# Twelve first sums of the down weights under gate and up, read-outs ordered ahead of sums, and plain rows loaded ahead, in a two-layer hybrid encoder

## The chip, the cores and the metric

The kernel runs on one core of one Trainium2 chip. The metric is device time in microseconds (us), the median of the runs; lower is better. In the profile PE is TensorE's matmul and PEld its weight load, DVE is VectorE, ACT is ScalarE, POOL is GpSimd and SP is SyncE, whose queue issues most of the DMAs.

## The reference

The reference is an encoder trunk of two layers on 1024 positions of width 1024, with 16 learned positions put in front (1040 in all). Each layer adds a mixer (a gated delta rule and a short convolution) and then a feed-forward block to the residual. The change lies in the feed-forward block alone:

```python
def swiglu(h, w_gate_up, w_down):
    gate, up = jnp.split(h @ w_gate_up.astype(h.dtype), 2, axis=-1)
    return (jax.nn.silu(gate) * up) @ w_down.astype(h.dtype)
```

Everything is float32. The inner width is 2816, which is 22 rows of 128. The last layer drops the 16 extra positions, so it works on 1024 columns where the first works on 1040.

## The kernel before, in words

**Three matmuls for one.** A float32 matrix is held as two fp32r parts: hi, a rounded copy that ACT makes, and lo, the value minus hi, which POOL makes for weights and DVE for activations. A product is three matmuls, hi by hi, hi by lo and lo by hi (lines 1064 to 1066 for gate and up, 1411 to 1413 for down).

**Seven products for eight.** Both matrix products of the feed-forward block use a Strassen form: the operands are cut into 2 x 2 blocks, and seven products of sums of blocks take the place of eight. For gate and up (the loop over the inner rows `f`, 0 to 21, line 1267) the four weight blocks A11, A12, A21 and A22 of a row are loaded, DVE forms the sums S1 to S4 from them (lines 1277 to 1282), `w_op` (lines 1042 to 1048) makes hi and lo of each, and PE runs p1 to p7. The products leave PSUM on ACT or DVE. Then POOL and DVE scale gate and up, ACT applies SiLU, DVE multiplies (line 1344), and the row goes to DRAM as `ad[f]` (line 1345).

**The down stage.** Down runs over the inner rows. The first four rows (`NF`) are plain: an ordinary product at the very end (`plain_row` prepares their activations, lines 1358 to 1365: load, hi on ACT at 1363, lo on DVE at 1364). The other 18 rows are two halves of nine (`NP`) and go through the seven products. Their work is written as 84 units: product P5, P3, P2, P1, P6, P7, P4 in this order, each with three blocks `b` of three inner rows and four output tiles `m`; a unit is one (product, b, m) with 18 matmuls in the first layer, whose 520 columns are done in two parts, and 9 in the second. A product's weights n = 4b + m are twelve tiles of 128 x 384.

The weights of four products are sums. They are formed in place in twelve half rows `S`:
- the first sum (S1, line 1150) adds two loaded tiles and serves P5;
- the second (S2, line 1152) subtracts a third tile, after P5's weight has been converted, and serves P3 (with one more subtraction, line 1181) and P6;
- the third (S3, line 1154) serves P7.

`s_raw` gives the home of sum n: rows that gate and up no longer need. `s_room` gives the eight half rows into which tiles for first and second sums are loaded: four rows, three that hold `up` and one that holds `gate` of the last products. `w_unit` (lines 1167 to 1186) converts the weight of a unit: hi on ACT (1184), lo on POOL (1185). `t_load` and `t_pair` do the same for the activations of a block (hi on ACT at 1229, lo on DVE at 1230; P7 and P4 need a subtraction first, at 1225 or 1228; at 1232 DVE updates a kept difference). `b_room` hands out seven half rows in turn for loaded activations, two neighbours for a plain row. Tiles with the tag `ck2` come from five buffers, which gate and up use for A21, A22 and two sums of each row and down for raw weights.

**Order.** What is emitted at which unit is written down in the list `under` (lines 1235 to 1247 and 1386 to 1387): weights five units ahead, activations some four, sums at units of their own, plain rows at units 37, 40, 43 and 46. First sums 0 to 7 are emitted by `s_under` behind products 8 to 15 of gate and up, first sums 8 to 11 at units 0 to 3. The emission order is a priority, not the order of execution: the framework simulates the engines' times and puts into each engine's queue, in order, what is ready first. So the first sums that are emitted from product 8 on run from 672.8 us on in the first layer, several products earlier, as soon as their rows are free. On the chip each queue then runs strictly in that order: an instruction that waits holds up all those behind it.

The products take eight PSUM banks in turn. P3 goes on in the banks of P5, P2 takes the next ones in the turn, P1 again the next, and P6, P7 and P4 go on in P1's. In the last block of a product, units 8 to 11 of its twelve, DVE adds the bank to the output rows (the read-out, line 1417), and the next product can write that bank only after it. These are the lines of a unit's end:

```python
                if b == NBK - 1:
                    dh, z, op = TO[p]
                    h = part(hr[4 * dh + m], z, j)
                    tt(out=h, in0=pin(ps), in1=h, op=op)
```

Of the kernel before, what the change touches and what calls it, by code (L numbers as in the profile page):

```python
# [7 lines left out]
F32 = mybir.dt.float32  # L8
# [12 lines left out]
FT = 22  # L21
# [21 lines left out]
def trunk(ctx: ExitStack, tc: tile.TileContext, xT, w_in, w_ba, w_out, w_gu, w_dn,  # L43
# [235 lines left out]
    for l in range(DEPTH):  # L279
# [834 lines left out]
        td = dram.tile([NP, 128, NB], F32, name=nm("td"))  # L1114
        dw = {}
        nr = [0, 0, 0]
        S_UP = 8

# [12 lines left out]
        def s_raw(n):  # L1131
            r = n // 2
            if ("S", r) not in dw:
                dw["S", r] = row(Y[1], F32, 3) if r < 3 else c4k("S") if r < 5 else row(Y[1] + "f")
            return dw["S", r][:, 384 * (n % 2):384 * (n % 2) + 384]

        def s_room():

            nr[2] += 1
            r = nr[2] // 2 % 4  # L1140
            if ("X", r) not in dw:
                dw["X", r] = row(X[1], F32, 3) if r < 3 else row(X[1] + "f")
            return dw["X", r][:, 384 * (nr[2] % 2):384 * (nr[2] % 2) + 384]

        def s_sum(which, n, room=None):

            S = s_raw(n)
            if which == "S1":
                r, o = room or (s_room(), s_room())
                tt(out=S, in0=a_load(r, 1, 0, n), in1=a_load(o, 1, 1, n), op=ALU.add)  # L1150
            elif which == "S2":
                tt(out=S, in0=S, in1=a_load(s_room(), 0, 0, n), op=ALU.subtract)
            else:
                tt(out=S, in0=a_raw(1, 1, n), in1=S, op=ALU.subtract)

        def s_under(f):

            n = f - 8
            if 0 <= n < S_UP:
                s_raw(n)  # L1160
                if n == 0:
                    s_raw(6)
                    s_raw(8)
                dw["S", 4]
                s_sum("S1", n, (dw["S", 4][:, 0:384], dw["S", 4][:, 384:768]))

        def w_unit(u):
# [9 lines left out]
            if p in ("P5", "P6", "P7"):  # L1177
                r = s_raw(n)
            elif p == "P3":
                r = a_raw(0, 1, n)  # L1180
                tt(out=r, in0=r, in1=s_raw(n), op=ALU.subtract)
            else:
                r = a_raw(*{"P2": (0, 1), "P1": (0, 0), "P4": (1, 1)}[p], n)
# [7 lines left out]
        def b_room(n=1):  # L1191

            if n == 2:
                nr[1] += nr[1] % 7 % 2
                if nr[1] % 7 == 6:
                    nr[1] += 1
            c0 = NB * (nr[1] % 7)
            nr[1] += n
            return dw["B"][:, c0:c0 + n * NB]
# [11 lines left out]
        def t_load(t):  # L1211
            p, i = SEVEN[t // NP], t % NP
            if p in BH:
                dw["b", t] = b_load(*BH[p], i)
            elif p == "P5":
                dma(t_raw(i), td[i])

        def t_pair(t):
            p, i = SEVEN[t // NP], t % NP
            hi, lo = t_slot(t)  # L1220
            r = dw.pop(("b", t), None)
            if p in ("P5", "P6"):
                r = t_raw(i)
            elif p == "P7":
                tt(out=r, in0=t_raw(i), in1=r, op=ALU.subtract)
            elif p == "P4":
                b21, r = r, t_raw(i)
                tt(out=r, in0=b21, in1=r, op=ALU.subtract)
            act(out=hi, in_=r, func=AF.Copy)
            tt(out=lo, in0=r, in1=hi.bitcast(F32), op=ALU.subtract)  # L1230
            if p == "P3":
# [5 lines left out]
        for n in range(12):  # L1237
            if n >= S_UP:
                under[n - 8].append(lambda n=n: s_sum("S1", n))
            under[n + 3].append(lambda n=n: s_sum("S2", n))  # L1240
            under[n + 46].append(lambda n=n: s_sum("S3", n))
        for t in range(4, NP * 7):
# [24 lines left out]
        for f in range(FT):  # L1267
# [16 lines left out]
            for n, a in ([("S3", A21), ("A22", A22), ("S4", s2t), ("A12", A12)] if end else  # L1284
                         [("S4", s2t), ("S3", A21), ("A12", A12), ("A22", A22)]):
                if f >= NE or n != "A12":
                    W[n] = w_op(a)
            g, u = early[f] if f < NE else (row((X[1], Y[1])[f % 2] + "f"), row(X[1], F32, 3))
            ps = {}
# [56 lines left out]
            if NF <= f < NF + NP:  # L1346
                tt(out=gv[:, 0:NB].rearrange("p (g e) -> p g e", g=2), in0=half(uv, 1), in1=half(uv, 0), op=ALU.subtract)
                dma(td[f - NF], gv[:, 0:NB])
            s_under(f)

# [5 lines left out]
        rest = []  # L1356

        def plain_row(f):

            u = b_room(2)  # L1360
            dma(u, ad[f][:, o0:L])
            lo = row(X[1], F32R, 3) if f < 3 else row(X[1] + "f", F32R)
            act(out=ax[:, f, o0:L], in_=u, func=AF.Copy)
            tt(out=lo[:, o0:L], in0=u, in1=ax[:, f, o0:L].bitcast(F32), op=ALU.subtract)
            rest.append((ax[:, f, :], lo))
# [20 lines left out]
        for i in range(NF):  # L1386
            under[37 + 3 * i].append(lambda i=i: plain_row(i))
        for u, (p, b, m) in enumerate(UNITS):
            if b == 1 and p in FIRST:
                dh, z = FIRST[p]  # L1390
                q = 4 * dh + m
                dma(half(hr[q][:, o0:L], z), half(hd[q][:, o0:L], z))
            for fn in under[u]:
                fn()
# [9 lines left out]
            for j in range(NJ):  # L1404
# [9 lines left out]
                if b == NBK - 1:  # L1414
                    dh, z, op = TO[p]
                    h = part(hr[4 * dh + m], z, j)
                    tt(out=h, in0=pin(ps), in1=h, op=op)

# [135 lines left out]
```

## Time and profile before

| | |
|---|---|
| runs | 2590.4, 2592.36 and 2598.9 us, median 2592.36 us |
| profiled execution | 2589.49 us, its span 2587.7 us |
| mean granted clock of TensorE | 0.991 |
| DMA | 360.04 MB, mean 139 GB/s |
| gate and up, first layer | from 610.1 us to about 1082 us |
| down, first layer | from 1081.7 us to about 1272 us |
| gate and up, second layer | from 1897.3 us to about 2346 us |
| down, second layer | from 2338.5 us to about 2529 us |

The profile is one execution, recorded by the hardware. The page gives the busy time of each engine over the span. The table by stretches cuts the span and gives for each stretch its length, each engine's busy time with the number of instructions in brackets, the clock that TensorE was granted (1.00 is full), the busy share of the DMA engines and the rate. The list of waits names the waiting instruction, the one that released it, the total, the number of times and the longest. In the timeline by engine a row has start, duration, engine, line, operation and tiles, and in square brackets how long the engine stood idle before it and what ended that. The groups by line give the shortest, the median and the longest duration in ns. Tile names show the buffer's tag: `a` and `b` are the large buffers and the rows `a3` and `b3`, `a3f` and `b3f` the fourth rows, `rw` the ck2 tiles, `S` the row of sums 8 and 9, `P` the buffers of split activations.

### The profile page before, as it was taken

To read this page: it belongs to the slowest core of one execution; us is meant where nothing else is said; L and a number is where in the kernel's file an instruction comes from. 1 tells how busy PE (TensorE), PEld (TensorE's weight loads), DVE (VectorE), ACT (ScalarE), POOL (GpSimd) and SP (SyncE) were. 2 spreads that over 40 slices of the span, in tenths; PEclk is the share of its full clock that TensorE was granted. 3 is DMA by queue.
4 is the path that set the end of the run, shared out by engine and by line. 5 is a ranking of instruction groups with operands and counts; after the bars stand their busy time and mean duration, and the time that the engine had idled before them with its cause. 6 is when DMAs were issued, how large, how long until landed. Compare 5 with 4: busy or idle time off the path is not lost. (4 is left out here: it accounts for less than half of the span.)

```text
span 2587.7 us, 45312 instructions
## 1 busy us (share of the span) xinstructions
PE 2504.7 (97%) x17508; PEld 2289.3 (88%) x17508; DVE 1640.2 (63%) x2461; ACT 1047.0 (40%) x1945; POOL 1134.3 (44%) x869
## 2 busy tenths in 40 slices
PE   8999999999899999999999989999989999999998
PEld 6989999998899999999998978999977778887787
DVE  4588433648766665778455874235587776668754
ACT  5563332435233333444445633324442333333444
POOL 2041212335666666665320302212456776774662
PEclk9999999999999999999999999999999999999999
DMA  3457265524422222674224582556343322228631
GB/s 127 128 184 266 92 206 167 186 78 124 131 98 87 96 83 81 212 221 144 78 92 134 189 269 77 181 159 204 106 133 115 111 88 92 89 82 276 202 109 66
DMA packets 213765, 360.04 MB, mean 139 GB/s; under 512 B 25461, under 2 KB 87869, under 8 KB 213549
## 3 DMA queue, kind: packets, MB, share of 16 engines
q1 hardware_dynamic: 180300, 310.17, 36.8%
q10 hardware_dynamic: 31072, 42.61, 5.4%
q0 software_dynamic: 2176, 4.36, 0.5%
q8 instruction: 137, 2.24, 0.4%
q14 instruction: 80, 0.65, 0.1%
HBM read 266.60 MB, written 90.46 MB: 138 GB/s over the span
## 5 line engine op out<-in xcount | busy, mean ns | idle before, releaser
L130 POOL TENSOR_TENSOR wlo<-raw,whi 128x512 fp32r<-128x512 f32 x132 | 177.5, 1346 | 770.2 <-ACT whi L129 698.4
L156 PE MATMUL pacc<-a,whi 128*128 128x346 f32 (+1 forms) x808 | 264.8, 331 | 9.9 <-ACT whi L129 8.3
L158 PE MATMUL pacc<-a,wlo 128*128 128x346 f32 (+1 forms) x808 | 264.5, 329 | 0.8 <-DVE wlo L130 0.8
L156 PE MATMUL pacc<-b,whi 128*128 128x346 f32 (+2 forms) x672 | 234.8, 350 | 0.0
L158 PE MATMUL pacc<-b,wlo 128*128 128x346 f32 (+2 forms) x672 | 232.5, 348 | 0.0
L157 PE MATMUL pacc<-a,whi 128*128 128x346 f32 (+1 forms) x688 | 227.0, 330 | 0.6 <-DVE a L177 0.3
L129 ACT ACTIVATE whi<-raw 128x512 fp32r<-128x512 f32 x168 | 105.2, 629 | 246.9 <-PE pacc L157 157.1
L157 PE MATMUL pacc<-b,whi 128*128 128x346 f32 (+2 forms) x580 | 200.5, 347 | 0.2 <-DVE b L905 0.2
L1047 POOL TENSOR_TENSOR wlo<-rw,whi 128x512 fp32r<-128x512 f32 x92 | 134.8, 1467 | 72.1 <-ACT whi L1046 66.8
L156 PEld LDWEIGHTS pacc<-a,whi 128*128 128x128 f32 x808 | 154.0, 191 | 13.9 <-ACT whi L129 10.2
L158 PEld LDWEIGHTS pacc<-a,wlo 128*128 128x128 f32 x808 | 154.1, 191 | 2.8 <-DVE wlo L130 1.4
L156 PEld LDWEIGHTS pacc<-b,whi 128*128 128x128 f32 x672 | 127.0, 189 | 11.4 <-issue 3.1
L157 PEld LDWEIGHTS pacc<-a,whi 128*128 128x128 f32 x688 | 131.8, 192 | 5.1 <-issue 2.9
L1047 POOL TENSOR_TENSOR a<-rw,a 128x512 fp32r<-128x512 f32 x64 | 105.6, 1651 | 69.7 <-ACT a L1046 69.0
L158 PEld LDWEIGHTS pacc<-b,wlo 128*128 128x128 f32 x672 | 126.9, 189 | 8.8 <-issue 0.8
L1047 POOL TENSOR_TENSOR b<-rw,b 128x512 fp32r<-128x512 f32 x64 | 92.6, 1449 | 84.2 <-ACT b L1046 50.2
L1046 ACT ACTIVATE whi<-rw 128x512 fp32r<-128x512 f32 x92 | 57.8, 630 | 144.5 <-DVE rw L1281 84.9
L157 PEld LDWEIGHTS pacc<-b,whi 128*128 128x128 f32 x580 | 109.6, 189 | 7.4 <-DVE b L905 0.5
L1282 DVE TENSOR_TENSOR rw<-raw,rw 128x512 f32<-128x512 f32 x44 | 97.2, 2209 | 1.2
L1277 DVE TENSOR_TENSOR rw<-rw,rw 128x512 f32<-128x512 f32 x44 | 67.5, 1533 | 47.3 <-POOL wlo L1047 30.9
L1047 POOL TENSOR_TENSOR wlo<-raw,whi 128x512 fp32r<-128x512 f32 x50 | 79.9, 1600 | 32.0 <-ACT whi L1046 21.3
L1046 ACT ACTIVATE b<-rw 128x512 fp32r<-128x512 f32 x64 | 40.2, 630 | 121.7 <-PE pacc L1065 35.2
(973 smaller groups left out, 8425.1 us busy)
## 6 DMA issues: line engine op xcount, KB each, us to landing
raw<-in_w_in SPq DMA_DIRECT2D x112, 256.0 KB
raw<-in_w_gu SPq DMA_DIRECT2D x104, 256.0 KB
rw<-in_w_gu SPq DMA_DIRECT2D x88, 256.0 KB
rw<-in_w_dn SPq DMA_DIRECT2D x86, 192.0 KB
rec<-aqd SPq DMA_DIRECT2D x62, 256.0 KB
rec<-vkd SPq DMA_DIRECT2D x61, 256.0 KB
raw<-in_w_out SPq DMA_DIRECT2D x48, 256.0 KB
b<-ad SPq DMA_DIRECT2D x45, 260.0 KB
```

Of the source, the lines that this page charges most:

```text
L129: act(out=hi, in_=raw[:, 0:kk, :], func=AF.Copy)
L130: (tt if lov[0] else ptt)(out=lo, in0=raw[:, 0:kk, :], in1=hi.bitcast(F32), op=ALU.subtract)
L156: mm(ps[:, :n], wh, xh[:, n0:n1], start=(k == 0), stop=False)
L157: mm(ps[:, :n], wh, xl[:, n0:n1], start=False, stop=False)
L158: mm(ps[:, :n], wl, xh[:, n0:n1], start=False, stop=(k == K - 1))
L1046: act(out=hi, in_=src, func=AF.Copy)
L1047: ptt(out=lo, in0=src, in1=hi.bitcast(F32), op=ALU.subtract)
L1277: tt(out=s1t, in0=A21, in1=A22, op=ALU.add)
L1282: tt(out=A21, in0=A11, in1=A21, op=ALU.subtract)
```

## The change

It has three parts.

**Twelve first sums under gate and up.** `s_under` is called in each product right after its weights have been prepared, before its matmuls are emitted, where it stood behind the product's end. Sums 8 and 9 are now emitted at products 16 and 17, sums 10 and 11 both at the last product, 21. Sums 8 to 11 load one tile into their own home and the other into a new `ck2` tile, where they took two rooms each. The home of sums 10 and 11 and the fourth row of rooms change places: the home is now the row that holds the gate of product 20 (`X[1] + "f"`), the rooms get the row of product 21's gate.

**Read-outs ahead of sums.** Each unit's read-out is remembered. `behind` adds to an operation of DVE that is emitted at unit u the condition that it runs after the read-out of unit u - 2, if that unit had one: to second and third sums, to the subtractions for P3's weights and for P7's and P4's activations, to the lo parts of activations and of plain rows. Units with a read-out are the last four of each product. Third sums are emitted three units later (n + 49 instead of n + 46).

**Plain rows loaded ahead.** A plain row's load is emitted three units ahead of its conversion, and the conversions stand at units 42, 44, 46 and 70 instead of 37, 40, 43 and 46. `held` keeps, for an assertion, which of the seven half rows are waiting to be read.

The diff, without the assertion's bookkeeping and the blank lines:

```diff
+        at, read_out = [0], {}
+        def behind(ins):
+            return after(ins, read_out.get(at[0] - 2))
-        S_UP = 8
@@ s_raw
-                dw["S", r] = row(Y[1], F32, 3) if r < 3 else c4k("S") if r < 5 else row(Y[1] + "f")
+                dw["S", r] = row(Y[1], F32, 3) if r < 3 else c4k("S") if r < 5 else row(X[1] + "f")
@@ s_room
-                dw["X", r] = row(X[1], F32, 3) if r < 3 else row(X[1] + "f")
+                dw["X", r] = row(X[1], F32, 3) if r < 3 else row(Y[1] + "f")
@@ s_sum
-                tt(out=S, in0=S, in1=a_load(s_room(), 0, 0, n), op=ALU.subtract)
+                behind(tt(out=S, in0=S, in1=a_load(s_room(), 0, 0, n), op=ALU.subtract))
-                tt(out=S, in0=a_raw(1, 1, n), in1=S, op=ALU.subtract)
+                behind(tt(out=S, in0=a_raw(1, 1, n), in1=S, op=ALU.subtract))
@@ s_under
-            n = f - 8
-            if 0 <= n < S_UP:
-                s_raw(n)
+            if f == FT - 1:
+                ns = (10, 11)
+            else:
+                ns = (f - 8,) if 0 <= f - 8 < 10 else ()
+            for n in ns:
+                S = s_raw(n)
                 if n == 0:
                     s_raw(6)
                     s_raw(8)
-                dw["S", 4]
-                s_sum("S1", n, (dw["S", 4][:, 0:384], dw["S", 4][:, 384:768]))
+                if n < 8:
+                    s_sum("S1", n, (dw["S", 4][:, 0:384], dw["S", 4][:, 384:768]))
+                else:
+                    s_sum("S1", n, (S, raw4("ck2").rearrange("p a b -> p (a b)")[:, 0:384]))
@@ w_unit, t_pair
-                tt(out=r, in0=r, in1=s_raw(n), op=ALU.subtract)
+                behind(tt(out=r, in0=r, in1=s_raw(n), op=ALU.subtract))
-                tt(out=r, in0=t_raw(i), in1=r, op=ALU.subtract)
+                behind(tt(out=r, in0=t_raw(i), in1=r, op=ALU.subtract))
-                tt(out=r, in0=b21, in1=r, op=ALU.subtract)
+                behind(tt(out=r, in0=b21, in1=r, op=ALU.subtract))
-            tt(out=lo, in0=r, in1=hi.bitcast(F32), op=ALU.subtract)
+            behind(tt(out=lo, in0=r, in1=hi.bitcast(F32), op=ALU.subtract))
@@ under
         for n in range(12):
-            if n >= S_UP:
-                under[n - 8].append(lambda n=n: s_sum("S1", n))
             under[n + 3].append(lambda n=n: s_sum("S2", n))
-            under[n + 46].append(lambda n=n: s_sum("S3", n))
+            under[n + 49].append(lambda n=n: s_sum("S3", n))
@@ gate and up: after the weights of product f, not after its end
+            s_under(f)
             g, u = early[f] if f < NE else (row((X[1], Y[1])[f % 2] + "f"), row(X[1], F32, 3))
...
-            s_under(f)
@@ plain rows
+        def plain_load(f):
+            dw["u", f] = b_room(2)
+            dma(dw["u", f], ad[f][:, o0:L])
         def plain_row(f):
-            u = b_room(2)
-            dma(u, ad[f][:, o0:L])
+            u = dw.pop(("u", f))
             lo = row(X[1], F32R, 3) if f < 3 else row(X[1] + "f", F32R)
             act(out=ax[:, f, o0:L], in_=u, func=AF.Copy)
-            tt(out=lo[:, o0:L], in0=u, in1=ax[:, f, o0:L].bitcast(F32), op=ALU.subtract)
+            behind(tt(out=lo[:, o0:L], in0=u, in1=ax[:, f, o0:L].bitcast(F32), op=ALU.subtract))
         for i in range(NF):
-            under[37 + 3 * i].append(lambda i=i: plain_row(i))
+            u = (42, 44, 46, 70)[i]
+            under[u - 3].append(lambda i=i: plain_load(i))
+            under[u].append(lambda i=i: plain_row(i))
@@ units
+            at[0] = u
-                    tt(out=h, in0=pin(ps), in1=h, op=op)
+                    read_out[u] = tt(out=h, in0=pin(ps), in1=h, op=op)
```

More of the change, by code (lines that the diff above doesn't have):

```diff
@@ L1114, in trunk @@
         td = dram.tile([NP, 128, NB], F32, name=nm("td"))
-        dw = {}
+        dw, held = {}, {}
+        at, read_out = [0], {}
+        def behind(ins):
+            return after(ins, read_out.get(at[0] - 2))
         nr = [0, 0, 0]
-        S_UP = 8
         def flat(tag, dt=F32):
@@ L1197, in b_room @@
             c0 = NB * (nr[1] % 7)
+            assert not [t for t, s in held.items() if c0 <= s < c0 + n * NB]
             nr[1] += n
@@ L1214, in t_load @@
                 dw["b", t] = b_load(*BH[p], i)
+                held[t] = NB * ((nr[1] - 1) % 7)
             elif p == "P5":
@@ L1221, in t_pair @@
             r = dw.pop(("b", t), None)
+            held.pop(t, None)
             if p in ("P5", "P6"):
@@ L1356, in trunk @@
         rest = []
+        def plain_load(f):
+            dw["u", f] = b_room(2)
+            dma(dw["u", f], ad[f][:, o0:L])
+            held["u", f], held["v", f] = (NB * ((nr[1] - i) % 7) for i in (1, 2))
         def plain_row(f):
-            u = b_room(2)
-            dma(u, ad[f][:, o0:L])
+            u = dw.pop(("u", f))
+            del held["u", f], held["v", f]
             lo = row(X[1], F32R, 3) if f < 3 else row(X[1] + "f", F32R)
             act(out=ax[:, f, o0:L], in_=u, func=AF.Copy)
-            tt(out=lo[:, o0:L], in0=u, in1=ax[:, f, o0:L].bitcast(F32), op=ALU.subtract)
+            behind(tt(out=lo[:, o0:L], in0=u, in1=ax[:, f, o0:L].bitcast(F32), op=ALU.subtract))
             rest.append((ax[:, f, :], lo))
```

## The prediction

> **What bounds the kernel now.** I read the page first: its span and the busy time of each engine.
>
> ```profile
> span 2587.7 us, 45312 instructions
> PE 2504.7 (97%) x17508; PEld 2289.3 (88%) x17508; DVE 1640.2 (63%) x2461; ACT 1047.0 (40%) x1945; POOL 1134.3 (44%) x869
> ```
>
> PE is the bound. The change removes no matmul, so all it can win is time in which PE waits, and the clock that PE loses behind a wait. I therefore asked next for the table by stretches, cut around the two down stages (the first layer's from 1081.6, the second's from 2338), and then for PE's waits in them.
>
> ```profile
> core 0: us, PE busy (x) PEld busy (x) DVE busy (x) ACT busy (x) POOL busy (x), PEclk, DMA share, GB/s
> 1081.60:1100.00 18.40, 18.40 (x156) 18.40 (x155) 15.25 (x21) 6.60 (x12) 9.07 (x5) 1.00 1.07 370
> 1100.00:1125.00 25.00, 22.58 (x182) 21.76 (x181) 24.35 (x36) 8.87 (x19) 13.02 (x11) 1.00 0.73 230
> 1125.00:1172.00 47.00, 47.00 (x396) 47.00 (x395) 27.84 (x38) 24.09 (x45) 30.59 (x25) 1.00 0.73 225
> 1188.00:1196.00 8.00, 4.93 (x29) 4.76 (x28) 8.00 (x15) 2.63 (x5) 2.45 (x2) 0.79 0.16 45
> 2338.00:2362.00 24.00, 24.00 (x105) 19.37 (x105) 21.78 (x30) 9.95 (x17) 11.71 (x7) 1.00 1.03 344
> 2366.00:2378.00 12.00, 7.96 (x23) 5.99 (x22) 9.42 (x15) 3.63 (x8) 4.99 (x5) 0.72 0.78 254
> 2450.00:2455.00 5.00, 3.60 (x16) 2.64 (x15) 5.00 (x9) 2.45 (x5) 2.32 (x2) 1.00 0.18 45
> 2455.00:2529.00 74.00, 74.00 (x319) 59.54 (x319) 43.33 (x52) 29.82 (x55) 42.78 (x41) 1.00 0.35 102
> ```
>
> ```profile
> PE pa L1411 <- ACT b L1184: 1.1, 1, 1.1
> PE pf L1411 <- ACT b L1184: 0.5, 1, 0.5
> PE pf L1413 <- POOL wlo L1185: 0.4, 1, 0.4
> PE pa L1413 <- POOL b L1185: 0.4, 1, 0.4
> ...
> PE pf L1411 <- DVE a L1417: 3.1, 1, 3.1
> ...
> PE pacc L1411 <- ACT a L1184: 4.0, 1, 4.0
> ...
> PE pa L1411 <- DVE b L1417: 1.4, 1, 1.4
> ```
>
> The first column pair of a stretch is its length and PE's busy time, so PE stands still 25.00 - 22.58 = 2.4, 8.00 - 4.93 = 3.1, 12.00 - 7.96 = 4.0 and 5.00 - 3.60 = 1.4 us: 10.9 us in all. The granted clock falls after two of them: 0.21 of 8 us is 1.7 us, 0.28 of 12 us is 3.4 us, together 5.1 us. So the down stages hold 16.0 us that this change can reach. The waits have two kinds of names. A hi part of a weight (L1184) is late: 1.1 and 0.5 us in the first layer, 4.0 us in the second. A read-out (L1417) is late, so that the bank cannot be used again: 3.1 and 1.4 us.
>
> A unit is 18 matmuls in the first layer (two column halves) and 9 in the second: 18 x 47.00/396 = 2.14 us and 9 x 74.00/319 = 2.09 us.
>
> **First sums.** Who makes the hi part late? The timeline around the 4.0 us, by engine:
>
> ```profile
> 2364.77 0.85 SPq L1124 DMA_DIRECT2D b<-in_w_dn  x2
> ...
> 2369.52 0.71 DVE L1150 TENSOR_TENSOR S<-b,b 128x384 f32<-128x384 f32 x1 [0.56 <-DMA b<-in_w_dn]
> 2370.16 0.55 DVE L1150 TENSOR_TENSOR a3f<-b,b3f 128x384 f32<-128x384 f32 x1
> ...
> 2370.27 0.52 ACT L1184 ACTIVATE a<-S 128x384 fp32r<-128x384 f32 x1 [1.57 <-DVE S L1150]
> ```
>
> The first sum of weight 9 is loaded at 2364.8, added at 2369.5 and converted at 2370.3 to 2370.8, when PE goes on; weight 11's sum, at 2370.2, is as late. Its load was late because first and second sums share eight half rows (rooms), which come free only as gate/up's last products are stored, and because DMA is full just then (shares of 1.07 and 1.03 in the rows at 1081.6 and 2338). The change takes sums 8 to 11 out of that queue. Sums 8 and 9 need their own half row and one ck2 tile and run under products 16 and 17. Sums 10 and 11 go into the row that holds product 20's gate, so they cannot start before that product's last multiply:
>
> ```profile
> 1067.74 1.73 DVE L1344 TENSOR_TENSOR a<-a,a3f 128x1040 f32<-128x1040 f32 x1
> ...
> 2336.50 1.23 DVE L1344 TENSOR_TENSOR b<-b,b3f 128x1024 f32<-128x1024 f32 x1
> ```
>
> That is 1069.5 and 2337.7, so "under gate and up" only just. Weight 10 is used as the eleventh of 2.09 us units, some 20 us after 2338; two loads and a sum fit. What is removed: 1.1 + 0.5 us in the first layer, with half of the two 0.4 us waits on POOL, which convert weights behind the same queue, makes 2.0 us; in the second layer 4.0 us and the 3.4 us of clock. That is 9.4 us. SP loses eight loads of 192 KB per layer in its crowded stretch and gets four of them between gate/up's weights, where the loads of the next product stand behind them.
>
> What do the added sums cost? The six to eight that already run under gate/up give the length.
>
> ```profile
> L1150 DVE TENSOR_TENSOR b<-S x6: 546/1140/1669, 672.8 to 709.6; 128x384 f32<-128x384 f32 x6
> L1150 DVE TENSOR_TENSOR a<-S x6: 546/1046/1675, 1961.4 to 2001.0; 128x384 f32<-128x384 f32 x6
> ```
>
> Eight more sums at a median of 1.1 us are 8.8 us of DVE, which is idle a third of the time. At best they fill gaps and cost nothing; at worst each delays a read-out by its longest duration, 8 x 1.675 = 13.4 us. I take 1.5 us, near the cheap end, since DVE has gaps of several microseconds in each product and four of the sums run beside the crowded stretch today anyway. Beside these rows stands a rule of the Trainium skill, "SBUF — State Buffer", section "SBUF: two separate sides": GpSimd and a VectorE operation on two SBUF inputs hold a shared port in turn, the loser waiting out the whole instruction. It speaks against this part, for POOL is busy with splits there; the spread from 546 to 1675 ns agrees. If every sum met POOL and PE waited for it, the rule would take 8 x (1.675 - 0.546) = 9.0 us instead of my 1.5, and the time would be 2586.5.
>
> **Read-outs ahead, plain rows ahead.** The 3.1 us wait, ACT and then DVE before it:
>
> ```profile
> 1176.29 0.32 SPq L1361 DMA_DIRECT2D b<-ad  x1
> ...
> 1179.76 1.07 ACT L1363 ACTIVATE a<-b 128x1040 fp32r<-128x1040 f32 x1 [5.54 <-DMA b<-ad]
> ...
> 1180.86 1.24 DVE L1364 TENSOR_TENSOR a<-b,a 128x1040 fp32r<-128x1040 f32 x1 [1.70 <-ACT a L1363]
> ...
> 1187.04 1.50 DVE L1230 TENSOR_TENSOR P<-b,P 128x520 fp32r<-128x520 f32 x1
> 1188.47 1.49 DVE L1225 TENSOR_TENSOR b<-b,b 128x520 f32<-128x520 f32 x1
> 1189.88 1.48 DVE L1230 TENSOR_TENSOR P<-b,P 128x520 fp32r<-128x520 f32 x1
> 1191.29 0.41 DVE L1417 TENSOR_TENSOR a<-pf,a 128x260 f32<-128x260 f32 x1
> ```
>
> A plain row's load is issued at 1176.3, ACT stands 5.5 us for it with weight conversions queued behind, DVE idles and then has its work in one lump, and the read-out comes last. The change loads a row three units (6.4 us) ahead, moves the fourth row from unit 46 to 70, starts the third sums three units later and orders the splits of units 46 to 49 (L1230) behind the read-outs of 44 to 47. Out of the lump ahead of this read-out go 1.24 + 1.50 + 1.48 = 4.2 us, more than the 3.1 it is late, besides the idle time. I count the 3.1 and its 1.7 us of clock in full and half of the second layer's 1.4, since the presums (L1225) and most third sums get no order: 5.5 us.
>
> The order itself adds waits. Behind a read-out on DVE now stand the splits, second sums and the differences for P3's weights; ACT, POOL and then PE wait for those. They are emitted about five units ahead of their use and released two units after the read-out's own, which leaves at least four units, 8 us, for operations of 0.5 to 1.5 us. I cost this at nothing; that cover gone, each product would wait a few microseconds. The fourth plain row at unit 70 puts 1.24 us on DVE where the row from 2455 shows it 43.33 of 74 us busy: nothing.
>
> **Sum.** 9.4 + 5.5 - 1.5 = 13.4 us. The profiled execution took 2589.5 us (its span and 1.8 us around it), so it would take 2576.1; it lies 2.9 us below the median of the runs, 2592.4, from which 2579.0 follows. The clock's part can be weighed too: the Trainium skill, "TensorE: Matmul & The Clock Gate", section on HAM oscillation, asks for no idle gap over about 3.4 us. By it the 3.1 us wait would keep full clock and the gain would be 11.7 us (2580.7); the row from 1188 shows 0.79, so here the trace decides.
>
> **Rivals.** (A) The read-outs stay late. Only operations emitted two units after a read-out are ordered, and in the last fence L1225 is not. Then the gain is 13.4 - 5.5 = 7.9 us: 2584.5. Against it: the 4.2 us counted above.
>
> (B) The 4.0 us wait moves on to P3's second block, unit 16.
>
> ```profile
> 2374.83 0.56 DVE L1152 TENSOR_TENSOR a<-a,b 128x384 f32<-128x384 f32 x1 [0.65 <-DMA b<-in_w_dn]
> ...
> 2375.89 0.52 ACT L1184 ACTIVATE whi<-raw 128x384 fp32r<-128x384 f32 x1 [4.63 <-DVE raw L1181]
> ...
> 2386.29 0.68 DVE L1230 TENSOR_TENSOR P<-a,P 128x512 fp32r<-128x512 f32 x1
> ```
>
> ACT stood 4.6 us for a second sum's load, and the block's last split ended at 2387.0. Without the wait PE would go on at 2370.8 - 4.0 = 2366.8 with units 9 and 11 and then four of P3, so unit 16 would start at 2366.8 + 6 x 2.09 = 2379.3 and want that split two thirds of a unit later, at 2380.7: it would be 6.3 us late if nothing else moved. For me speaks that the second sums get the rooms which the first sums held. Price: 13.4 - 6.3 = 7.1 us of gain, 2585.3.
>
> (C) Slower: the extra ck2 tiles of products 16 and 17 hold up gate/up's own loads.
>
> ```profile
> DVE rw L1277 <- DMA rw<-in_w_gu: 15.2, 6, 3.8
> ...
> 2240.76 0.68 DVE L1277 TENSOR_TENSOR rw<-rw,rw 128x512 f32<-128x512 f32 x1
> ...
> 2249.79 1.30 POOL L1047 TENSOR_TENSOR wlo<-rw,whi 128x512 fp32r<-128x512 f32 x1 [0.27 <-ACT whi L1046]
> ```
>
> Five ck2 tiles serve four uses per product, and the sum of A21 and A22 (L1277) already waits for loads, up to 3.8 us. With the fifth tile taken, PE would wait at four places (two products, two layers), 3.8 us and 1.7 us of clock each: 22 us against 13.4, 2601. It decides only if the load is over 8 us late: the sum at 2241.4 is converted on POOL from 2249.8, when its weight slot comes free. That cover speaks against it.
>
> (D) The planner, which simulates times to order each queue, leaves the queues as they were, or spends the gain by a new order elsewhere: 2590.
>
> **How the numbers follow.** 0.3%, 7.8 us, is about what a measurement of this kernel can tell from no change. My forecast has 0.57, A 0.14, B 0.14, C 0.09, D 0.06. Faster takes the forecast, half of A and 0.04 of B: 0.68; slower is C, 0.09; 0.23 remain. The low end, 2573, is all 16.0 us at no cost and some 3 us that a new order may save elsewhere; the high end, 2589, takes in A, B and the rule's 2586.5. D and C lie beyond it.
>
> **What would show it.** In the changed profile: PE's waits on L1184 gone from both down stages and the stretch of 12 us at full clock; the first-sum line (L1150 here) ending before the down units begin but for two sums per layer; no wait on a read-out over 1 us; ACT idle at the plain rows under 1 us; gate/up no more than 1 us longer per layer. I am wrong if PE waits at unit 16 or behind the third sums as long as it did, or if products 17 and 18 show new waits on L1277's chain.

## The result and the profile after

The changed kernel took 2581.07 us, the median of 7 runs (2573.41 to 2584.82), against 2592.36 us for the kernel before (7 runs, 2588.77 to 2598.9). The medians lie 11.3 us apart. The ratio of the runs is 0.9949, with a 95% interval from 0.9934 to 0.9963; by it the kernel is 13.2 us faster (9.6 to 17.1), more than the 0.3% that a measurement of this kernel can tell from no change.

The profiled execution took 2583.93 us. From its page, the span and the engines:

```profile
span 2582.2 us, 45315 instructions
PE 2501.5 (97%) x17508; PEld 2285.0 (88%) x17508; DVE 1651.3 (64%) x2461; ACT 1046.1 (41%) x1945; POOL 1139.5 (44%) x869
```

The number of matmuls is unchanged, as are DVE's instructions. The table by stretches, over the places where the kernel before stood still, and then over both down stages as a whole (they begin at 1084.8 and 2338.0 here):

```profile
core 0: us, PE busy (x) PEld busy (x) DVE busy (x) ACT busy (x) POOL busy (x), PEclk, DMA share, GB/s
1100.00:1125.00 25.00, 24.29 (x203) 24.08 (x203) 24.44 (x39) 8.25 (x16) 9.67 (x9) 1.00 0.78 258
1188.00:1200.00 12.00, 10.77 (x87) 10.37 (x87) 12.00 (x17) 4.33 (x9) 5.67 (x6) 1.00 0.36 101
2374.00:2380.00 6.00, 3.73 (x17) 2.72 (x16) 2.51 (x6) 1.04 (x2) 5.34 (x4) 1.00 0.40 117
...
1084.80:1269.50 184.70, 181.82 (x1510) 180.80 (x1510) 135.39 (x182) 76.54 (x142) 102.53 (x80) 1.00 0.57 176
2338.00:2521.80 183.80, 181.09 (x776) 145.25 (x775) 131.06 (x158) 80.88 (x149) 112.58 (x92) 1.00 0.60 188
```

The same two stretches in the profile of the kernel before:

```profile
1081.70:1270.60 188.90, 183.42 (x1511) 182.42 (x1510) 130.66 (x182) 76.79 (x142) 100.06 (x80) 0.99 0.56 175
2338.50:2528.30 189.80, 184.13 (x777) 147.29 (x776) 133.94 (x162) 81.42 (x149) 109.51 (x92) 0.98 0.60 188
```

The clock is full throughout, and the down stages are 4.2 and 6.0 us shorter: 10.2 us. What is still lost shows in PE's waits, those in the first layer's first blocks, those in the rest of that layer, and the second layer's two:

```profile
PE pa L1431 <- DVE P L1243: 0.7, 1, 0.7
PE pacc L1430 <- DVE a L1339: 0.2, 1, 0.2
...
PE pacc L1430 <- DVE a L1436: 0.8, 1, 0.8
PE pf L1431 <- DVE P L1243: 0.7, 1, 0.7
PE pb L1430 <- DVE a L1436: 0.4, 1, 0.4
...
PE pacc L1432 <- POOL a L1195: 2.3, 1, 2.3
...
PE pa L1431 <- DVE P L1243: 0.4, 1, 0.4
```

(The change moves the lines: the matmuls stand at 1430 to 1432, the read-out at 1436, a weight's hi and lo at 1194 and 1195, an activation's lo at 1243, the sums at 1155, 1157 and 1159, P3's difference at 1191, a plain row's load, hi and lo at 1371, 1379 and 1380.)

No wait on a hi part (line 1194) is left. A new one is there: 2.3 us on POOL's lo of a weight, in P3. Gate and up, from their first matmul to the first of down, took 470.8 and 441.4 us, against 471.6 and 441.2 before: the added sums cost nothing that shows in this profile. Between the two kernels' first gate matmul lies another 3.8 us (613.9 against 610.1 us), in a stretch whose code is the same; the other profiles below have 607 to 613 us there.

### The profile page after: what moved, and what is told of

The parts are those of the page before. It is cut to its first block, busy times and chain, and to the rows that moved or that the text cites. A ratio compares the mean times of both kernels' runs of the same rounds, so it can differ in the third digit from the quotient of the medians.

```text
span 2582.2 us, 45315 instructions
## 1 busy us (share of the span) xinstructions
PE 2501.5 (97%) x17508; PEld 2285.0 (88%) x17508; DVE 1651.3 (64%) x2461; ACT 1046.1 (41%) x1945; POOL 1139.5 (44%) x869
## 4 chain that ended last, share of the span: by engine, by line
PE 52%; DVE 10%; DMA 4%; issue 3%; POOL 2%; ACT 1%; SPq 0%; ACTq 0%; DVEq 0%; POOLq 0%
PE pacc L156 5%; PE pacc L158 5%; PE pacc L157 5%; PE pacc L1064 3%; PE pacc L1066 3%; PE pacc L1065 3%; PE pb L1064 2%; PE pb L1065 2%; PE pb L1066 2%; PE pf L1064 2%; PE pf L1066 2%; PE pf L1065 2%; PE pacc L1432 1%; PE pacc L1430 1%; PE pacc L1431 1%
## 5 line engine op out<-in xcount | busy, mean ns | idle before, releaser
L156 PEld LDWEIGHTS pacc<-b,whi 128*128 128x128 f32 x672 | 127.4, 190 | 11.3 <-issue 3.1
```

Of the source, the lines that this page charges most:

```text
L156: mm(ps[:, :n], wh, xh[:, n0:n1], start=(k == 0), stop=False)
```

## The experiments

The theory with which they began: the sums and the read-outs give what was forecast, and the order takes part of it back at P3, because DVE's operations now stand there in one train and POOL's splits come late. Rivals: the sums alone give all of it and the order nothing; the plain rows, not the order, move the waits.

**The sums alone.** No order, third sums and plain rows where they were, but for the fourth plain row: it stays at unit 70, since its row is the home of sums 10 and 11.

```diff
-            return after(ins, read_out.get(at[0] - 2))
+            return ins
-            under[n + 49].append(lambda n=n: s_sum("S3", n))
+            under[n + 46].append(lambda n=n: s_sum("S3", n))
-            u = (42, 44, 46, 70)[i]
-            under[u - 3].append(lambda i=i: plain_load(i))
+            u = (37, 40, 43, 70)[i]
+            under[u].append(lambda i=i: plain_load(i))
```

> The changed kernel without the order behind read-outs, with third sums at n + 46 again and each plain row loaded where it is converted, at units 37, 40, 43 and 70 (the fourth stays at 70, since its row is the home of sums 10 and 11). My theory: the two parts add up, each in its own stretch. Then the first 20 units are as in the changed kernel (no wait on a hi part in the first layer, 2 to 3 us at P3's second block in the second), and the wait on a read-out where P6 begins is back: 2.5 to 3.5 us and one half-clock window in the first layer, 1 to 2 us in the second. Down stages 187 to 188 us and 184 to 186 us, time 6 to 9 us under the kernel before. Rival: the order behind read-outs is what clears the first block too (it puts the splits of P3 behind P5's read-outs); then the second layer shows a wait of 4 us or more in the first 20 units and the time is less than 4 us under the kernel before.

Measured: 2586.95 us (12 runs), ratio to the kernel before 0.9978 (0.9966 to 0.9989), 5.7 us faster. In the first blocks one wait of 0.5 us is left, on a lo part in the first layer, but the waits on a read-out, in the first and in the second layer, read:

```profile
PE pf L1430 <- DVE a L1436: 1.8, 1, 1.8
...
PE pa L1430 <- DVE b L1436: 5.8, 1, 5.8
```

The second was 1.4 us before the change. With the 4-us stall gone, PE arrives at P6 105.9 us after the stage's first matmul instead of 113.5, but it can go on only at 111.7 us instead of 114.9, since the read-out has come forward by 3.1 us alone: the wait has moved on, and 6.8 us at half clock (from 2440.9 us) follow it. DVE's timeline at that place shows what the read-out stands behind:

```profile
2439.29 1.48 DVE L1243 TENSOR_TENSOR P<-a,P 128x512 fp32r<-128x512 f32 x1
2440.69 1.47 DVE L1238 TENSOR_TENSOR a<-a,a 128x512 f32<-128x512 f32 x1
2442.09 0.68 DVE L1243 TENSOR_TENSOR P<-a,P 128x512 fp32r<-128x512 f32 x1
2442.69 0.54 DVE L1159 TENSOR_TENSOR a<-rw,a 128x384 f32<-128x384 f32 x1
2443.16 0.68 DVE L1436 TENSOR_TENSOR b<-pa,b 128x512 f32<-128x512 f32 x1
```

**Everything but the sums.** First sums, homes and rooms as before; order, third sums and plain rows as changed. Not shown are the lines that give the homes, the rooms and the call of `s_under` their old places.

```diff
-            if f == FT - 1:
-                ns = (10, 11)
-            else:
-                ns = (f - 8,) if 0 <= f - 8 < 10 else ()
+            ns = (f - 8,) if 0 <= f - 8 < 8 else ()
...
+            if n >= 8:
+                under[n - 8].append(lambda n=n: s_sum("S1", n))
```

> The other half: homes, rooms and first sums as in the kernel before (eight under gate and up, four at units 0 to 3), but with the order behind read-outs, third sums at n + 49 and plain rows loaded ahead at units 42, 44, 46 and 70. My theory: the wait on weight 9 stays, about 4 us and 3.4 us of lost clock in the second layer and 1.6 us in the first; the wait on read-outs where P6 begins is as in the changed kernel, under 1.5 us in each layer. Down stages about 186 us and 188 to 189 us, time 3 to 6 us under the kernel before. Rival: the new order puts more on DVE ahead of the late first sums, so that the first block waits longer than in the kernel before, and this half alone gains nothing.

Measured: 2593.65 us (11 runs), ratio 1.0006 (0.9994 to 1.0017): no gain. PE's waits in the second layer:

```profile
PE pacc L1429 <- ACT a L1191: 4.4, 1, 4.4
PE pa L1431 <- POOL wlo L1192: 3.5, 1, 3.5
```

(Lines 1191 and 1192 are hi and lo here.) The 4-us wait on weight 9's sum is back, and behind it, in P3, stands a wait on POOL's lo that neither the kernel before nor the sums alone have: that split took 5.57 us, from 2384.34 us. So the parts do not add up: 5.7 us for the one, nothing for the other, 13.2 together. The sums move the second layer's wait to P6, and only versions with the order have it short there.

**The sums and the plain rows, without the order.**

```diff
-            return after(ins, read_out.get(at[0] - 2))
+            return ins
```

> The changed kernel without the condition behind read-outs alone; third sums stay at n + 49, plain rows at 42, 44, 46 and 70 with loads ahead. My theory: the condition is what shortened the wait where P6 begins, so it is back at 2 us or more in the first layer; first down stage 186 to 188 us against 184.8. Rival: the later third sums and the fourth plain row's move did it, and the wait stays under 1.5 us; down stages within 1 us of the changed kernel's 184.8 and 183.8 us.

Measured: 2586.57 us (5 runs), ratio 0.9971 (0.9955 to 0.9986). P6's waits are as with the sums alone, and P3 has none:

```profile
PE pf L1430 <- DVE a L1436: 2.1, 1, 2.1
...
PE pa L1430 <- DVE b L1436: 4.5, 1, 4.5
```

Later sums and shifted plain rows do not by themselves bring the read-outs in time; with the rows at these units the order is needed. That is read from the waits of one profile each: the intervals of this version and of the changed kernel overlap.

**The plain rows loaded with their conversion.**

```diff
-            under[u - 3].append(lambda i=i: plain_load(i))
+            under[u].append(lambda i=i: plain_load(i))
```

> The changed kernel with each plain row's load emitted at the unit of its conversion instead of three units ahead. My theory after seeing the changed profile: loading ahead does nothing, since the third row's load is issued at 1177.2 us, as late as the last in the kernel before (1176.3), because its buffer is still read; so the down stages stay within 1 us of 184.8 and 183.8 us and ACT waits as long for the rows (25 us in all). Rival: the earlier emission keeps the loads from being later still; then ACT waits over 30 us and the wait where P6 begins grows by 1 us or more.

Measured: 2577.37 us (4 runs), ratio 0.9942 (0.9926 to 0.9958), not to be told from the changed kernel's 0.9949. The wait at P3 is there as well:

```profile
PE pacc L1432 <- POOL a L1195: 2.6, 1, 2.6
```

Loading ahead gave nothing. Why, the changed kernel's own rows say. The idle time of ACT before a plain row's conversion, in the kernel after:

```profile
  DMA b<-ad: 15.4, 4
  DMA a<-ad: 9.7, 4
```

and in the kernel before:

```profile
  DMA b<-ad: 9.1, 4
  DMA a<-ad: 4.8, 4
```

It went up, from 13.9 to 25.1 us over the eight rows; 10.2 us of the 25.1 are the two fourth rows, which now stand at unit 70. With the loads at their conversions it is 22.0 us, not the 25 that were expected. The third row's load is emitted earlier but not issued earlier. SP's waits between 1150 and 1190 us and the third row's load:

```profile
SPq L1371 <- DVE P L1243: 5.3, 2, 3.3
...
SPq L1371 <- DVE a L1436: 2.6, 1, 2.6
```

```profile
1177.18 0.32 SPq L1371 DMA_DIRECT2D b<-ad  x1
```

The half row into which a load goes is still to be read by an activation's split (line 1243), and SP stands for that split or for a read-out. The kernel before has the same waits in this stretch, 4.7 us on the split and 2.7 us on read-outs, and issued its last plain load at 1176.3.

**The order from P2 on.** No operation that is emitted before unit 24 waits for a read-out any more, so the order at P5's and P3's hand-over is gone.

```diff
-            return after(ins, read_out.get(at[0] - 2))
+            return after(ins, read_out.get(at[0] - 2) if at[0] >= 24 else None)
```

> The changed kernel with the order behind read-outs only from unit 24 on (P2 and later); P5's read-outs order nothing. My theory: the order behind P5's read-outs packs DVE's work of the first block into one train without a gap, in which POOL gets no turn (one split took 6.86 us at 2369.6 us of the changed profile), and PE waits 2.3 us for it. Then the waits of 2.4 us in the second layer and 0.9 us in the first (near unit 15 to 17) go, POOL's longest split there is under 3 us, and the waits where P6 begins stay under 1.5 us: down stages about 184 and 181.5 us, 2 to 4 us less than the changed kernel. Rival: PE then comes to P6 earlier and the wait moves on to P6's first unit, as it did with the sums alone; down stages as in the changed kernel, no gain.

Measured: 2574.88 us (6 runs), ratio 0.9936 (0.9924 to 0.9949). No wait of PE in a down stage is over 0.5 us, and POOL's splits of weights near the place of the 2.3 us (groups by line, 2360 to 2385 us) are short:

```profile
L1195 POOL TENSOR_TENSOR a<-rw,a x7: 1012/1461/2462, 2359.5 to 2384.3; 128x384 fp32r<-128x384 f32 x7
```

**Both edits.**

```diff
-            return after(ins, read_out.get(at[0] - 2))
+            return after(ins, read_out.get(at[0] - 2) if at[0] >= 24 else None)
...
-            under[u - 3].append(lambda i=i: plain_load(i))
+            under[u].append(lambda i=i: plain_load(i))
```

> The same, with each plain row's load emitted at its conversion's unit. My theory: where the load is emitted makes no difference of its own, so the time is within 3 us of that of the kernel with the late order alone, and the first down stage is 181 to 185 us. Rival: loading ahead takes the neighbouring half rows from the activations of P6 and P7 and so costs about 3 us in the first layer (184.8 against 181.7 us in the earlier pair); then this kernel is 3 us or more faster than the one with the late order alone, mostly in the first layer.

Measured: 2577.04 us (5 runs), ratio 0.9937 (0.9924 to 0.9950), with waits in the down stages of 0.5, 0.5 and 1.1 us. The late order alone does as well, so loading ahead does not cost the 3 us of the rival.

**P3's first splits on DVE instead of POOL.** This tests whether POOL itself is the bottleneck at P3.

```diff
-            ptt(out=lo, in0=r, in1=hi.bitcast(F32), op=ALU.subtract)
+            (tt if 15 <= u < 19 else ptt)(out=lo, in0=r, in1=hi.bitcast(F32), op=ALU.subtract)
```

> The changed kernel with the lo parts of the weights of units 15 to 18 made by DVE instead of POOL, all else the same. If POOL is starved by DVE's train, the wait on POOL at unit 15 of the second layer (2.3 us) goes to under 1 us, though DVE has four more operations. If instead the weight is late because its difference stands late on DVE, behind the read-outs, the wait stays at 2 us or more and is then on DVE.

Measured: 2578.88 us (4 runs), ratio 0.9953 (0.9936 to 0.9969). The waits in the second layer change their name:

```profile
PE pacc L1432 <- DVE a L1195: 2.3, 2, 1.5
PE pf L1432 <- DVE a L1195: 1.7, 1, 1.7
```

At unit 15, the place of the 2.3 us, PE now waits 0.7 us, as expected if POOL was starved. But 1.7 and 1.5 us follow within three units, behind loads for which DVE stood 3.5 and 2.4 us, and the first layer has a new wait of 1.5 us at unit 15, so the move gains nothing: 4.0 us on DVE in the second layer take the place of 2.3 on POOL. DVE's split at unit 15 is the last operation of its train (2376.67 us), about as late as POOL was with it. The one split that POOL keeps at this place takes 7.76 us; the read-out ahead of it on DVE stands first:

```profile
2369.78 0.69 DVE L1436 TENSOR_TENSOR b<-pacc,b 128x512 f32<-128x512 f32 x1
2370.32 7.76 POOL L1195 TENSOR_TENSOR a<-rw,a 128x384 fp32r<-128x384 f32 x1 [9.32 <-ACT a L1194]
```

**The third plain row later as well.** The order from unit 24 on, and the third row at unit 66.

```diff
-            return after(ins, read_out.get(at[0] - 2))
+            return after(ins, read_out.get(at[0] - 2) if at[0] >= 24 else None)
...
-            u = (42, 44, 46, 70)[i]
+            u = (42, 44, 66, 70)[i]
```

> The kernel with the late order, and the third plain row converted at unit 66 instead of 46. In the changed kernel ACT stood 5.4 us for that row's load with weights and splits behind it, and DVE's lump just after it holds the read-outs that PE waited 1.2 us for in the first layer. My theory: without the row there, ACT's wait before P6 goes and the waits where P6 begins fall under 0.5 us in both layers; first down stage 182 to 183 us. Rival: the lump is made of third sums and presums that meet POOL, not of the row; then the waits stay at 1 us or more.

Measured: 2572.32 us (5 runs, 2571.5 to 2573.57), ratio 0.9924 (0.9912 to 0.9936): the lowest median of all, some 20 us under the kernel before and 6 to 9 under the changed one. Its interval overlaps that of the late order alone (0.9924 to 0.9949), so what the third row adds to it is not told apart. The first layer's down stage (1082.7 to 1264.0 us) took 181.3 us, with one wait of 0.5 us in P5. In the second layer's down stage PE does not wait at all:

```profile
2328.80:2509.40 180.60, 180.60 (x777) 145.44 (x776) 137.37 (x157) 81.01 (x149) 112.15 (x92) 1.00 0.61 192
```

**Its two edits, one by one.** The third row at unit 66 with the full order:

```diff
-            u = (42, 44, 46, 70)[i]
+            u = (42, 44, 66, 70)[i]
```

> The changed kernel with only one edit: the third plain row at unit 66 instead of 46; every added order stays, early products' too. If the gain of the best version is two separate gains (order released from unit 24 on about 6 us, third row late about 3 us), this one takes only the second: 2577 to 2579 us, ratio 0.994 to 0.9945 to the kernel before, with the wait of about 2.3 us on POOL's split at P3's weight in the second layer still there and no wait in the first layer's P6. Rival: the waits at P3 come from the place of the row as well, and this version is as good as the best, 2572 us (0.9924), with no wait at unit 15.

Measured: 2578.6 us (4 runs), ratio 0.9933 (0.9913 to 0.9953). The wait at P3 in the second layer is gone, against the first expectation, although the order is in full force there; one of 1.3 us on a lo part stands in the first layer's P3.

The third row at unit 66 without any order:

```diff
-            return after(ins, read_out.get(at[0] - 2))
+            return ins
...
-            u = (42, 44, 46, 70)[i]
+            u = (42, 44, 66, 70)[i]
```

> The third plain row at unit 66, and no added order at all. If the order from unit 24 on is what keeps P6's read-outs in time, they are late here as they were without any order (2.3 us in the first layer, 4.6 us and a half-clock window in the second): about 2584 us, ratio 0.997. Rival: P6's read-outs were late because the plain rows stood ahead of them, and with the third row gone from there the order is no longer needed: 2573 us, ratio 0.9925, and no wait over 1 us.

Measured: 2578.97 us (4 runs), ratio 0.9939 (0.9922 to 0.9956), between the two expectations. The first layer's P6 no longer waits, where it waited 2.1 us with the row at unit 46, so there the plain row was what stood ahead of the read-out. In the second layer it does:

```profile
PE pa L1430 <- DVE b L1436: 3.2, 1, 3.2
```

with 6.8 us at half clock after it. There the order is still needed; the third row's place alone takes the wait from 4.5 to 3.2 us.

**The wait at P3: the queue or the execution?** The version with the full order and a late third row has the changed kernel's operations at P3 in the same sequence on DVE, and no stall; its read-out and its split:

```profile
2368.48 0.69 DVE L1436 TENSOR_TENSOR b<-pacc,b 128x512 f32<-128x512 f32 x1
2368.73 1.01 POOL L1195 TENSOR_TENSOR a<-rw,a 128x384 fp32r<-128x384 f32 x1 [10.43 <-ACT a L1194]
```

So the theory that the order makes the stall was in doubt, and the two kernels were profiled once more, unedited.

> The changed kernel once more, unedited, for a second profile of it. Theory: POOL's split in the second layer's P3 loses by the order in which the planner queues DVE's work, so every execution shows it: a split of 6 to 8 us near 2370 us and a wait of PE of 2 to 2.7 us on it, as in three profiles so far. Rival: DVE's queue is the same as in the version with the third row at unit 66, whose split got through in 1.44 us, and chance in the arrival decides: then this profile may show no split over 3 us there and no wait over 1 us at that place, and the down stage of the second layer is about 2.3 us shorter than 183.8.

> The version with the third plain row at unit 66 and the full order once more, unedited. Theory: its queue lets the split through, so again no split over 3 us near 2370 us and no wait over 1 us in the second layer's P3. Rival: chance decides, and it may show a split of 6 to 8 us with a wait of 2 to 2.7 us this time.

Measured: 2575.22 and 2568.9 us, one run each. The late third row has no wait in the second layer again, and one of 0.9 us in the first layer's P3. The changed kernel has no stall this time. PE's longest wait in either of its down stages is 0.5 us, and these are 182.7 and 182.4 us long:

```profile
1080.30:1263.00 182.70, 181.73 (x1511) 180.86 (x1510) 134.76 (x182) 76.68 (x142) 102.58 (x80) 1.00 0.57 177
2331.20:2513.60 182.40, 181.85 (x777) 144.86 (x776) 136.47 (x158) 80.94 (x149) 107.28 (x92) 1.00 0.61 190
```

The same split of the same kernel, first in the group of the first profile (two splits, shortest, median and longest) and in its timeline (the two together), with DVE's rows beside it:

```profile
L1195 POOL TENSOR_TENSOR a<-rw,a x2: 987/3922/6856, 2369.6 to 2376.4; 128x384 fp32r<-128x384 f32 x2
```

```profile
2369.59 7.81 POOL L1195 TENSOR_TENSOR a<-rw,a 128x384 fp32r<-128x384 f32 x2 [9.62 <-ACT a L1194]
```

```profile
2368.62 0.69 DVE L1436 TENSOR_TENSOR b<-pacc,b 128x512 f32<-128x512 f32 x1
2369.22 0.55 DVE L1157 TENSOR_TENSOR S<-S,b 128x384 f32<-128x384 f32 x1
...
2374.91 0.68 DVE L1245 TENSOR_TENSOR a<-a 128x512 f32<-128x512 f32 x1
```

and then the second profile, DVE and POOL:

```profile
2362.20 0.69 DVE L1436 TENSOR_TENSOR b<-pacc,b 128x512 f32<-128x512 f32 x1
2362.80 1.36 DVE L1157 TENSOR_TENSOR S<-S,b 128x384 f32<-128x384 f32 x1
```

```profile
2362.73 1.02 POOL L1195 TENSOR_TENSOR a<-rw,a 128x384 fp32r<-128x384 f32 x1 [10.18 <-ACT a L1194]
2365.87 1.44 POOL L1195 TENSOR_TENSOR a<-rw,a 128x384 fp32r<-128x384 f32 x1 [2.12 <-ACT a L1194]
```

In the second execution the split is issued 0.53 us after the read-out's start and done in 1.02 us, and DVE's next sum takes 1.36 instead of 0.55 us. In the first it is issued 0.97 us after the read-out's start, when that sum is already running, and ends only behind DVE's last operation of the train, 6.86 us later. So the rival holds for the changed kernel: the same program has the stall in one execution and not in the other. Six profiles have this sequence on DVE, and the arrival of the split, counted from the start of the read-out (pacc, line 1436) ahead of it, parts them: at 0.25, 0.33 and 0.53 us it got through in 1.0 us (the late third row twice, the changed kernel's second profile), at 0.54, 0.65 and 0.97 us it took 7.76, 7.17 and 6.86 us (the splits on DVE, the late loads, the changed kernel's first). The next operation of DVE, with two inputs in SBUF where the read-out has one, starts 0.60 us after the read-out. The two nearest arrivals, one on each side, lie only 0.01 us apart, and one of them is of another program (the splits on DVE); so where the edge lies, and whether the arrival alone decides, six profiles do not show, and it was not tried by itself. That DVE's queue makes the stall possible is better founded: of seven profiles with the full order four have waits on lo parts in the second layer's P3 (2.3, 2.6 and 3.5 us, and 4.0 us with the splits on DVE) and three have none, and none of the six with the late order or no order has one.

## Why the prediction was right, and where not

**The total.** 13.4 us were forecast. By the ratio of the runs it is 13.2 us (9.6 to 17.1), by the medians 11.3; the down stages give 10.2 us in the first profile and 378.7 - 365.1 = 13.6 in the second. The mechanism was right: PE was kept waiting by late first sums and late read-outs, and now the sums are no longer late and the read-outs by 0.8 us at most. That the number came so close is in part luck: 1.5 us were booked for the added sums, which took none here, nothing for the order, which took up to 3.0 us at P3, and the two profiles of this one program lie 8.7 us apart (2583.93 and 2575.22; 2576.1 was forecast for the profiled execution).

**First sums, forecast 9.4 us.** In the first layer the first blocks' waits went from 2.4 us to at most 0.9: 1.5, for a forecast of 2.0. In the second the 4.0 us and the 3.4 us of clock are gone in every version that has the twelve sums, and are back in the one without. What the working missed is what is late next: with the sums alone 5.8 us and a half-clock stretch appear at P6. The gain of 9.4 us was real only together with the order, which the prediction had as a separate term of 5.5.

**Read-outs, forecast 5.5 us.** 3.1 us and 1.7 of clock became 0.8 + 0.4 us in the first profile and no wait on a read-out in the second; the second layer's 1.4 us became 0.4, and the wait has another name. Of 6.2 us that is 4.6 gained in the first profile and, with one wait of 0.5 us left in the second layer, 5.7 in the second. The size was right, and the part is worth more than it was given: without the order the second layer's wait is now 3.2 to 5.8 us. Rival A, read-outs that stay late, is out.

**Added sums, forecast 1.5 us of cost.** The eight sums of weights 8 to 11 read, in the groups by line of the first profile:

```profile
L1155 DVE TENSOR_TENSOR S<-S,rw x4: 544/558/559, 949.8 to 2235.3; 128x384 f32<-128x384 f32 x4
L1155 DVE TENSOR_TENSOR a3f<-a3f,rw x2: 550/555/560, 1078.7 to 1079.5; 128x384 f32<-128x384 f32 x2
L1155 DVE TENSOR_TENSOR b3f<-b3f,rw x2: 1375/2068/2762, 2342.0 to 2344.6; 128x384 f32<-128x384 f32 x2
```

Six of eight took the shortest time, and the two long ones lie at the start of down, where PE did not stand. Gate and up changed by -0.8 and +0.2 us. The sum by the rule on the shared port, 9.0 us, did not come about here, and rival C (gate and up's loads held up) is out. In the changed kernel the term was zero, in its second profile too (470.6 us in the first layer). Whether it is zero in every order of the queues is open: in seven of the other versions with the twelve sums the first layer's gate and up took 472.3 to 474.3 us. Six of them have a wait of 0.3 to 0.9 us in the last product, three 3.4 us at half clock near 680 us; whether the sums cause either is not shown.

**"The order itself adds waits ... I cost this at nothing."** This is the step that failed. In the first profile P3's split came 2.3 us late in the second layer, and the first layer's two waits of 0.7 us are on lo parts, which the order holds back. One of the two stands in P3, and a wait of 0.3 to 1.3 us stands there in all five profiles with the full order, the twelve sums and the splits on POOL, and in none with the late order or no order. The cover of four units that the prediction named was counted in DVE's own durations of 0.5 to 1.5 us; a split on POOL that takes 6.86 us was not among the rows from which it was worked out. The profile before held a hint, a split of 3.80 us on POOL at 2354.7 us, for which no matmul waited. At P3 the order's price is 0.4 us in the second profile and 3.0 us in the first, by the execution. The late order, which takes this away, measured 0.9936 against 0.9949, with intervals that overlap.

**Rival B,** a wait that moves on to P3, was near: unit 15 instead of 16, POOL's split instead of a second sum's load, 2.3 us in place of 6.3, and not every time.

**Plain rows loaded ahead: wrong in its check, without weight in the sum.** ACT's idle time at plain rows was to be under 1 us; it is 25.1 us over eight rows, as shown above. What took waits away was moving rows from the read-outs: with the third row at unit 66 the first layer's P6 waits for nothing even without the order.

What stays open: why a split that comes in the middle of DVE's train can get in (1.44 us, in the second profile) where another waits for its end. And the single profile of the kernel before may itself be one of several courses; its runs (2588.77 to 2598.9) were not taken apart.

## What to carry to other kernels

A wait that is removed gives its time only as far as the next hand-over that was late too and was covered by it: work out when PE will arrive there, before adding up gains by place. A load that is emitted earlier is issued earlier only if its buffer is free earlier; look at what the queue of loads waits for. And a wait that depends on two engines' contest can be absent from the next execution of the same program: profile a kernel twice before a cause is given to a wait of two microseconds.

## What the runs showed of the hardware

A subtraction of 128x384 on POOL, 1.02 us when it comes through, took 6.86, 7.17 and 7.76 us beside an unbroken run of DVE operations that mostly have two inputs in SBUF. Each of the three ended 0.85 to 0.86 us after the last operation of that run. The Trainium skill, "SBUF — State Buffer", section "SBUF: two separate sides", has the loser of the shared port wait for the whole instruction. The 1.36 us of DVE's sum beside a 1.02 us split agrees with that; the 6.86 us, eleven of DVE's operations, go beyond it. That the port is the cause is argued from the coincidence; no run isolates it.

Half clock (a granted clock of 0.50) for 3.4 us followed waits of PE of 2.1 us (the version without the order, first layer), 2.6 (late loads) and 3.1 us (before), and 6.8 us of it one of 3.2 us (the late third row without any order); waits of 1.8 (sums alone) and 2.3 us (after) had none. One and the same wait shows both: PE stands 2.1 us near 680 us, in the first layer's gate and up, in eight of the profiles, and in three of them 3.4 us at half clock follow (the late order, the splits on DVE, the late order with the late third row), in the other five, the kernel before among them, none. The Trainium skill, "TensorE: Matmul & The Clock Gate", section on HAM oscillation, allows gaps up to about 3.4 us; by these rows the edge here lies lower, and it is not one sharp length.
